# A staged first quarter in stages of 1, 2, 2, 3, 4 and 4 k tiles, with one modulation chunk lent a weight buffer

## The chip, the cores and the metric

One core of a Trainium2 chip runs the kernel. The metric is the device time of one execution in microseconds (us). The profile and the trace come from one profiled execution.

## What is computed

One layer of a flow-matching trunk over 128 context tokens and 256 latent tokens, all in fp32 with D = 2048. Nine modulation vectors per token kind come from `silu(c) @ w_ada + b_ada`; two feed-forward halves stand around a mixer:

```python
def swiglu_sublayer(x, g, w_gate, w_up, w_down, shift, scale, gate):
    h = rms_norm(x, g) * (1 + scale) + shift
    f = (jax.nn.silu(h @ w_gate) * (h @ w_up)) @ w_down
    return x + 0.5 * gate * f

m_ctx = adaln(c_ctx, w_ada[l], b_ada[l])
m_lat = [m[:, None, :] for m in adaln(c, w_ada[l], b_ada[l])]
x_ctx = swiglu_sublayer(x_ctx, ffn1_norm[l], ffn1_w_gate[l], ffn1_w_up[l], ffn1_w_down[l],
                        m_ctx[0], m_ctx[1], m_ctx[2])
...
x_ctx = mixer_output(x_ctx, a, gm, out_norm_a[l], out_norm_b[l], w_out[l], m_ctx[5])
x_ctx = swiglu_sublayer(x_ctx, ffn2_norm[l], ffn2_w_gate[l], ffn2_w_up[l], ffn2_w_down[l],
                        m_ctx[6], m_ctx[7], m_ctx[8])
```

The latent tokens go the same way with neighbourhood attention. Everything that the change touches lies in the first feed-forward half, and there in the first 250 us.

## The kernel before

**Products.** Tokens (384) are the moving columns, with two more columns that carry the shift while the row norm is not known yet (386). Each fp32 product is done as three: weights are split into a high part `whi` (a cast on ACT, line 250) and a low part `wlo` (a subtraction on DVE, line 251), activations into `hh` and `hl`, and `three` (lines 279 to 284) issues `wlo x hh`, `whi x hl`, `whi x hh` into one accumulation bank. A weight chunk W is 1 MB; its two halves are split and used one after the other. A half holds two k tiles of 128 rows by four output columns of 128, so 24 products. I call the n-th half of the kernel slot n, from 0 on. Four pairs of `whi` and `wlo` exist (`NWP`), three buffers `raw` for chunks from HBM (`NRAW`).

**Modulation.** The shift and scale of the first norm (vectors 0 and 1) have to be known before `hh` can be made. They come from 32 chunks A of `w_ada`, 1 MB each, multiplied on TensorE with `silu(c)` as 32-column weights (`ada_chunk`, line 345). When all chunks of a unit of k tiles are through, DVE copies the sums (line 352), four-column products turn them into columns (`ada_unit`, line 364), DVE adds the bias (369) and makes the scale (388), ACT makes `hh` (`raw_hi`, 502) and DVE `hl` (`raw_lo`, 507). Chunks A have two buffers `rawa` (`NADA`) and, at the start, two of the `raw` buffers.

**The staged quarter** (`first_quarter_staged`). Of the hidden columns of the first feed-forward half, the first quarter has six groups. So that products can start before all modulation is known, they run in stages over k tiles (`BLOCKS`, line 39): (0, 2), (2, 4), (4, 6), (6, 8), (8, 12), (12, 16). In each stage all six groups are multiplied with the stage's k tiles. Each group has four accumulation banks of the five of the pool `acc`; at the end of a group's stage `after` evicts them: in the first stage by copies, alternately on ACT (line 720) and DVE (718), in later stages by additions on DVE to the partial sums (724). Before the first slot four chunks A are done; behind each of slots 0 to 27 one more (`ADA_AFTER`, lines 773 and 774), and the columns of a finished unit follow behind the next slot (`settle`).

**What sets the order.** Each engine runs its instructions in the order of the program. `half` (line 262) first splits weights ahead, then runs what `later` has put at this slot's number: loads of x (line 1166), the squares for the row norm (`squares`, lines 1168 and 1169: four squares on ACT and, on DVE, additions to `ssq`, line 455) at slots 9, 12, 16 and 22, the norm at 24. `pump` (line 183) issues loads in the order of use as buffers come free: weight chunks and the first six chunks A on SP's queue, later chunks A on POOL's. A load on a queue that waits for its buffer holds up those behind it.

Of the kernel before, what the change touches and what calls it, by code (L numbers as in the profile page):

```python
# [8 lines left out]
F32 = mybir.dt.float32  # L9
# [6 lines left out]
P = 128  # L16
D = 2048
KT = D // P
# [6 lines left out]
CW = 512  # L25
CK = 4
# [12 lines left out]
BLOCKS = ((0, 2), (2, 4), (4, 6), (6, 8), (8, 12), (12, 16))  # L39
NPE = 0  # L40
ADA_UNITS = tuple(((0, k0, k1), (1, k0, k1)) for k0, k1 in BLOCKS) + ((tuple((2, k, k + 4) for k in range(0, NPE, 4)),) if NPE else ())
ADA_AFTER = (1,) * (28 + NPE)
NSEL = 4

# [70 lines left out]
class Kernel:  # L115
# [4 lines left out]
    def setup(self):  # L120
# [28 lines left out]
        self.freed = {"W": 0, "A": 0}  # L149
        self.next_split = 0  # L150
# [6 lines left out]
        self.room = 2  # L157
# [25 lines left out]
    def pump(self):  # L183

        nc = self.nc
        room = {"W": self.room, "A": NADA}
        while True:
            can = [self.order[k][n] for k, n in self.issued.items()
                   if n < min(len(self.order[k]), self.freed[k] + room[k])]
            if not can:  # L190
                return
            c = min(can)
            k = self.kinds[c]
            if k == "A":
                raw = self.start.tile([P, CK * CW], F32, tag="rawa", name="rawa", bufs=NADA)
                src = self.a["wada_s"][self.issued[k]]
            else:
                raw = self.wp.tile([P, CK * CW], F32, tag="raw", name="raw", bufs=NRAW)
                src = self.a["ws"][self.issued[k]]
            (nc.gpsimd if k == "A" and self.issued[k] >= 6 else nc.sync).dma_start(out=raw, in_=src)  # L200
            self.raw[c] = raw
            self.issued[k] += 1

    def first_loads(self):

        nc = self.nc
        na = 2 * BLOCKS[0][1]
        xin = lambda k, n: nc.sync.dma_start(out=self.xall[:, k:k + n, :], in_=self.a["xT"][:, k:k + n, :])  # L210
        cols = CK * CW
        order = self.order["A"][:na - 1] + [self.order["W"][0], self.order["A"][na - 1]]
        for c in order:
            k = self.kinds[c]
            i = self.issued[k]
            if k == "A" and i < NADA:
                raw = self.start.tile([P, cols], F32, tag="rawa", name="rawa", bufs=NADA)
            else:
                raw = self.wp.tile([P, cols], F32, tag="raw", name="raw", bufs=NRAW)
            self.raw[c] = raw  # L220
            self.issued[k] += 1
            src = self.a["wada_s" if k == "A" else "ws"][i]
            if k == "W":
                w_raw, w_src = raw, src
                nc.sync.dma_start(out=raw[:, 0:1024], in_=src[:, 0:1024])
            elif i < na - 1:
                nc.sync.dma_start(out=raw, in_=src)
                if i == 1:
                    nc.sync.dma_start(out=self.par, in_=self.a["par"])
                    xin(0, 2)  # L230
            else:
                for c0 in range(0, cols, 512):
                    nc.sync.dma_start(out=raw[:, c0:c0 + 512], in_=src[:, c0:c0 + 512])
                nc.sync.dma_start(out=w_raw[:, 1024:cols], in_=w_src[:, 1024:cols])
                self.lent = set(self.order["A"][NADA:na])
        self.freed["A"] = na - NADA
        self.freed["W"] = NADA - na
# [19 lines left out]
    def done(self, c):  # L257
        del self.raw[c]
        self.freed["W" if c in self.lent else self.kinds[c]] += 1
        self.pump()  # L260
# [65 lines left out]
    def ada_chunk(self):  # L326
# [16 lines left out]
        for q in range(nsub):  # L343
# [3 lines left out]
                             stop=done and q >= nsub - 4, tile_position=(0, r))  # L347
        self.done(c)
# [355 lines left out]
    def first_quarter_staged(self):  # L704
# [38 lines left out]
        for st, (k0, k1) in enumerate(BLOCKS):  # L743
            for pairs in stage_halves(st):
# [4 lines left out]
                if slot == 0:  # L749
                    for kk, u in order:  # L750
                        if kk == 0:
                            banks[pairs[0][0], u] = self.bank(u)
                    for w, x, i in ((hi, self.hh, 0), (hi, self.hl, 1), (lo, self.hh, 2)):
                        for kk, u in order:
                            w0 = kk * CW + u * P
                            nc.tensor.matmul(banks[pairs[0][0], u][:, :TS], lhsT=w[:, w0:w0 + P],  # L756
                                             rhs=x[:, kk, :], start=i == 0 and kk == 0, stop=i == 2 and kk == 1)
                    for u in range(4):
                        after(st, pairs[0][0], u, banks.pop((pairs[0][0], u)))
                    order = []  # L760
                for kk, u in order:
# [362 lines left out]
    def run(self):  # L1124
# [15 lines left out]
        with ExitStack() as st:  # L1140
# [3 lines left out]
            self.ada_rows()  # L1144
            self.first_loads()
            xin = lambda k, n=4: nc.sync.dma_start(out=self.xall[:, k:k + n, :], in_=a["xT"][:, k:k + n, :])
            self.gh, self.gl = {}, {}
            for _ in range(2 * BLOCKS[0][1] - 1):
                self.ada_chunk()
            self.ahead(1)  # L1150
            self.ada_chunk()
            self.settle()
            self.ahead(2)
            self.pump()
            xin(2, 2)
# [10 lines left out]
            for k, sl in ((4, 6), (8, 12), (12, 18)):  # L1166
                self.later(sl, lambda k=k: xin(k))
# [3 lines left out]
            one = [(2, k) for k in range(NPE, KT)] + [(j, k) for j in (3, 4) for k in range(KT)]  # L1171
# [11 lines left out]
            self.later(31 + NPE, switch)  # L1183
# [188 lines left out]
```

## Time and profile before

| | |
|---|---|
| median of 3 runs | 2826.48 us (2826.29 to 2827.67) |
| time of the profiled execution | 2826.2 us |
| its span, first to last instruction | 2824.1 us |
| PE busy | 2797.0 us (99%) |
| PE's weight loads (PEld) | 2711.1 us (96%) |
| DVE, ACT, POOL busy | 65%, 36%, 7% |
| mean granted clock of TensorE | 0.997 of full |
| HBM read | 511.88 MB, 185 GB/s over the span |

In the profile's rows a line starts with its start and its busy time in microseconds; `out<-in` are the program's tiles; in brackets stands the idle time ahead of it on its engine and what ended it. L345 is line 345 of the kernel before. PE is TensorE's products, PEld its weight loads, SPq and POOLq the queues that issue transfers. A matmul of fp32 tiles stands as two pieces, so x16 at line 345 are eight products; products overlap, so the distance of their starts counts, not their length.

### The profile page before, as it was taken

The page shows a single profiled execution, that of the slowest core. Times are in us where ns is not written, and L with a number is a line of the kernel's source. Part 1 is how long each engine was busy: PE and PEld are TensorE (multiplying, and loading weights), DVE is VectorE, ACT ScalarE, POOL GpSimd, SP SyncE. Part 2 cuts the span into 40 slices and gives each one's busy share as a digit, 9 for nine tenths or more (in the row PEclk, how much of TensorE's full clock was granted, in tenths as well). Part 3 has the DMA queues.
Part 4 walks back from the last instruction along what each step waited for, and adds up shares of the span by engine and source line. Part 5 has one row for each costly group of instructions (what it writes and reads, how often), then busy time and mean ns, then how long its engine had stood idle before and what let it go on. Part 6 is the DMA issues. An engine that isn't in the chain of part 4 may idle for free.

```text
span 2824.1 us, 39182 instructions
## 1 busy us (share of the span) xinstructions
PE 2797.0 (99%) x15984; PEld 2711.1 (96%) x15984; DVE 1841.8 (65%) x2887; ACT 1015.3 (36%) x1454; POOL 187.4 (7%) x302
## 2 busy tenths in 40 slices
PE   8999999999999999999999999999999999999997
PEld 6889999999999999988888999999999999999997
DVE  4767889798999798765566877554444543333335
ACT  3345432322322244543344445333333223322342
POOL 0031011011111010000000000000000000000000
PEclk9999999999999999999999999999999999999999
DMA  8854676666667675454333653444444433333432
GB/s 349 311 190 166 219 251 240 237 239 241 250 241 253 246 257 197 147 170 141 125 120 116 256 222 137 149 159 162 165 155 151 163 127 129 125 121 138 157 132 80
DMA packets 100035, 524.89 MB, mean 186 GB/s; under 512 B 11024, under 2 KB 18832, under 8 KB 55056
## 3 DMA queue, kind: packets, MB, share of 16 engines
q1 hardware_dynamic: 62224, 371.39, 36.0%
q0 software_dynamic: 37632, 151.01, 15.6%
q8 instruction: 125, 2.05, 0.3%
q14 instruction: 54, 0.44, 0.0%
HBM read 511.88 MB, written 10.49 MB: 185 GB/s over the span
## 4 chain that ended last, share of the span: by engine, by line
PE 99%; DVE 0%; DMA 0%; SPq 0%; ACT 0%; issue 0%; DVEq 0%
PE acc L282 24%; PE acc L284 24%; PE acc L283 24%; PE mp L282 7%; PE mp L284 7%; PE mp L283 6%; PE acc L307 2%; PE acc L308 2%; PE acc L309 2%; PE mp L345 1%; PE mp L858 0%; PE mp L908 0%; PE mp L938 0%; DMA raw<-wada_s 0%; DVE x L1240 0%; PE acc L756 0%
## 5 line engine op out<-in xcount | busy, mean ns | idle before, releaser
L251 DVE TENSOR_TENSOR wlo<-raw,whi 128x1024 fp32r<-128x1024 f32 x640 | 784.5, 1227 | 808.5 <-ACT whi L250 808.1
L250 ACT CAST whi<-raw 128x1024 fp32r<-128x1024 f32 x640 | 670.6, 1050 | 1425.0 <-PE mp L284 1149.9
L282 PE MATMUL acc<-hh,wlo 128*128 128x384 f32 (+1 forms) x2744 | 933.5, 340 | 0.0
L284 PE MATMUL acc<-hh,whi 128*128 128x384 f32 (+1 forms) x2744 | 927.6, 338 | 0.0
L283 PE MATMUL acc<-hl,whi 128*128 128x384 f32 (+1 forms) x2744 | 925.6, 337 | 0.0
L282 PEld LDWEIGHTS acc<-hh,wlo 128*128 128x128 f32 x2744 | 516.6, 188 | 25.5 <-issue 11.3
L283 PEld LDWEIGHTS acc<-hl,whi 128*128 128x128 f32 x2744 | 518.0, 189 | 0.8
L284 PEld LDWEIGHTS acc<-hh,whi 128*128 128x128 f32 x2744 | 516.6, 188 | 0.0
L282 PE MATMUL acc<-gh,wlo 128*128 128x384 f32 x1056 | 357.6, 339 | 0.0
L283 PE MATMUL acc<-gl,whi 128*128 128x384 f32 x1056 | 354.3, 336 | 0.0
L284 PE MATMUL acc<-gh,whi 128*128 128x384 f32 x1056 | 352.8, 334 | 0.0
L436 DVE CUSTOM_DVE_ANT_0 scr<-adaw,csb,par 128x1024 bf16<-128x1024 f32 x224 | 287.3, 1282 | 4.4
L436 DVE CUSTOM_DVE_ANT_0 scr<-adaw,csb,m 128x1024 bf16<-128x1024 f32 x224 | 287.3, 1282 | 4.2
L284 PE MATMUL mp<-hh,whi 128*128 128x384 f32 (+1 forms) x704 | 237.8, 338 | 0.0
L282 PE MATMUL mp<-hh,wlo 128*128 128x384 f32 (+1 forms) x704 | 237.2, 337 | 0.0
L283 PE MATMUL mp<-hl,whi 128*128 128x384 f32 (+1 forms) x704 | 237.0, 337 | 0.0
L421 POOL DMA_DIRECT2D adaw<-wada_t x224 | 118.5, 529 | 1447.9 <-DVE m L436 1352.8
L284 PEld LDWEIGHTS acc<-gh,whi 128*128 128x128 f32 x1056 | 198.5, 188 | 0.0
L283 PEld LDWEIGHTS acc<-gl,whi 128*128 128x128 f32 x1056 | 198.3, 188 | 0.0
L282 PEld LDWEIGHTS acc<-gh,wlo 128*128 128x128 f32 x1056 | 198.0, 188 | 0.0
L283 PEld LDWEIGHTS mp<-hl,whi 128*128 128x128 f32 x704 | 132.7, 189 | 0.0
L282 PEld LDWEIGHTS mp<-hh,wlo 128*128 128x128 f32 x704 | 132.5, 188 | 0.0
(170 smaller groups left out, 2238.5 us busy)
## 6 DMA issues: line engine op xcount, KB each, us to landing
raw<-ws SPq DMA_DIRECT2D x319, 1024.0 KB, 4.9
adaw<-wada_t POOLq DMA_DIRECT2D x224, 512.0 KB, 4.0
rawa<-wada_s POOLq DMA_DIRECT2D x26, 1024.0 KB, 5.9
csb<-crow POOLq DMA_DIRECT2D x6, 1024.0 KB, 7.9
keep<-x SPq DMA_DIRECT2D x8, 768.0 KB, 6.8
rawa<-wada_s SPq DMA_DIRECT2D x4, 1024.0 KB, 8.7
bias<-bias SPq DMA_DIRECT2D x16, 256.0 KB, 4.9
xo<-xT SPq DMA_DIRECT2D x16, 192.0 KB, 5.5
```

The costliest lines, as they stand in the source:

```text
L250: nc.scalar.copy(hi, src)
L251: nc.vector.tensor_sub(lo, src, hi.bitcast(F32))
L282: nc.tensor.matmul(o, lhsT=wl, rhs=xh, start=first, stop=False)
L283: nc.tensor.matmul(o, lhsT=wh, rhs=xl, start=False, stop=False)
L284: nc.tensor.matmul(o, lhsT=wh, rhs=xh, start=False, stop=last)
L307: nc.tensor.matmul(o, lhsT=xh, rhs=wl, start=first and kk == 0, stop=False)
L308: nc.tensor.matmul(o, lhsT=xl, rhs=wh, start=False, stop=False)
L309: nc.tensor.matmul(o, lhsT=xh, rhs=wh, start=False, stop=last and kk == 1)
L345: nc.tensor.matmul(self.ada_bank[r:r + 32, :cols], lhsT=self.csil[:, nsub * kc + q, w0:w0 + 32], rhs=raw[:, q * cols:(q + 1) * cols], star ...
L421: self.nc.gpsimd.dma_start(out=t, in_=self.a["wada_t"][j - 2, kt, kh])
L436: nc.vector.tensor_tensor_reduce(out=scr, in0=t, in1=self.csb[:, v, :], scale=1.0, scalar=init, op0=ALU.mult, op1=ALU.add, accum_out=acc)
```

## The change

Stages are now (0, 1), (1, 3), (3, 5), (5, 8), (8, 12), (12, 16). Units of modulation are the same ranges, with the fourth cut in two, (5, 6) and (6, 8). Only two chunks A come before slot 0; two follow each of slots 0 and 1, none slot 2, and one each of slots 3 to 28. Stage one has one k tile, so that a half holds two groups, each with three products a bank; stage four has three, so that by turns a half holds two k tiles of one group, the last of one and the first of the next, and two of the next. A finished unit's columns are settled in the middle of the next half, behind its fourth triple. The fifth chunk A (A4, counted from 0) goes into one of the three `raw` buffers, which now are taken from a list of free ones; the weight chunks have one buffer of room at the start instead of two. x is loaded in smaller pieces. Around the first chunks `fill` issues products of `ones` into a bank that nobody reads: five behind A0, one behind each quarter of A1, four behind the columns.

```diff
-BLOCKS = ((0, 2), (2, 4), (4, 6), (6, 8), (8, 12), (12, 16))
-NPE = 0
-ADA_UNITS = tuple(((0, k0, k1), (1, k0, k1)) for k0, k1 in BLOCKS) + ((tuple((2, k, k + 4) for k in range(0, NPE, 4)),) if NPE else ())
-ADA_AFTER = (1,) * (28 + NPE)
+BLOCKS = ((0, 1), (1, 3), (3, 5), (5, 8), (8, 12), (12, 16))
+UNITS = ((0, 1), (1, 3), (3, 5), (5, 6), (6, 8), (8, 12), (12, 16))
+LENT = 4
+ADA_UNITS = tuple(((0, k0, k1), (1, k0, k1)) for k0, k1 in UNITS)
+ADA_AFTER = (2, 2, 0) + (1,) * 26
+FILL = (5, 1, 1, 4)
...
-        self.room = 2
+        self.room = 1
...
-            can = [self.order[k][n] for k, n in self.issued.items()
-                   if n < min(len(self.order[k]), self.freed[k] + room[k])]
+            can = [self.order[k][n] for k, n in self.issued.items() if n < len(self.order[k]) and
+                   (self.free if k == "A" and n == LENT else
+                    n - (k == "A" and n > LENT) < self.freed[k] + room[k] and (k == "A" or self.free))]
...
+            if k == "A" and self.issued[k] == LENT:
+                raw = self.raw_buf(c)
+                src = self.a["wada_s"][self.issued[k]]
...
             elif i < na - 1:
                 nc.sync.dma_start(out=raw, in_=src)
-                if i == 1:
-                    nc.sync.dma_start(out=self.par, in_=self.a["par"])
-                    xin(0, 2)
+                xin(0, 1)
             else:
+                nc.sync.dma_start(out=self.par, in_=self.a["par"])
                 for c0 in range(0, cols, 512):
...
+    def fill(self, n):
+        for _ in range(n):
+            self.nc.tensor.matmul(self.idle[:, :P], lhsT=self.ones, rhs=self.ones, start=True, stop=True)
...
+            if (q + 1) % (nsub // 4) == 0 and q < nsub - 1:
+                self.fill(between)
...
                 if slot == 0:
-                    for kk, u in order:
-                        if kk == 0:
-                            banks[pairs[0][0], u] = self.bank(u)
+                    for u in range(4):
+                        banks[pairs[0][0], u] = self.bank(u)
                     for w, x, i in ((hi, self.hh, 0), (hi, self.hl, 1), (lo, self.hh, 2)):
-                        for kk, u in order:
-                            w0 = kk * CW + u * P
-                            nc.tensor.matmul(banks[pairs[0][0], u][:, :TS], lhsT=w[:, w0:w0 + P],
-                                             rhs=x[:, kk, :], start=i == 0 and kk == 0, stop=i == 2 and kk == 1)
+                        for u in range(4):
+                            nc.tensor.matmul(banks[pairs[0][0], u][:, :TS], lhsT=w[:, u * P:(u + 1) * P],
+                                             rhs=x[:, 0, :], start=i == 0, stop=i == 2)
...
-                    order = []
-                for kk, u in order:
+                    order = order[4:]
+                for at, (kk, u) in enumerate(order):
+                    if at == 4:
+                        self.settle()
...
-            for _ in range(2 * BLOCKS[0][1] - 1):
+            for n in FILL[:2 * BLOCKS[0][1] - 1]:
                 self.ada_chunk()
+                self.fill(n)
             self.ahead(1)
-            self.ada_chunk()
+            self.ada_chunk(FILL[-3])
+            self.fill(FILL[-2])
             self.settle()
+            self.fill(FILL[-1])
             self.ahead(2)
+            self.room = 2
             self.pump()
-            xin(2, 2)
+            xin(1, 2)
...
-            for k, sl in ((4, 6), (8, 12), (12, 18)):
-                self.later(sl, lambda k=k: xin(k))
+            for k, n, sl in ((3, 2, 2), (5, 3, 5), (8, 4, 11), (12, 4, 17)):
+                self.later(sl, lambda k=k, n=n: xin(k, n))
```

The order in which instructions stand moves at three places of the staged quarter.

First, SP's queue behind the loads of the start, before (`rawa` and `wada_s` are chunks A, `ws` weight chunks; the first two rows are A4 and A5, then W1 and W2):

```order
L200 DMA rawa<-wada_s 128x2048 [waits DMAHW4_49,PE_49]
L200 DMA rawa<-wada_s 128x2048 [waits DMAHW5_49,PE_49]
L200 DMA raw<-ws 128x2048 [waits DMAHW6_49,PE_49]
L200 DMA raw<-ws 128x2048 [waits DMAHW2_49,DMAHW1_49,DMAHW7_49,DMAHW0_49,PE_49]
L1146 DMA x<-xT 128x768
L200 DMA raw<-ws 128x2048 [waits DMAHW3_49,DVE_49]
```

and with the change (A2, A3, A4, W1, W2, x, W3, A5, W4):

```order
L211 DMA rawa<-wada_s 128x2048 [waits DMAHW2_49,PE_49]
L211 DMA rawa<-wada_s 128x2048 [waits DMAHW5_49,DMAHW6_49,DMAHW3_49,DMAHW7_49,DMAHW0_49,PE_49]
L211 DMA raw<-wada_s 128x2048 [waits DMAHW4_49]
L211 DMA raw<-ws 128x2048
L211 DMA raw<-ws 128x2048 [waits DMAHW1_49,DVE_49]
L1171 DMA x<-xT 128x768
L211 DMA raw<-ws 128x2048 [waits DMAHW5_49,DVE_49]
L211 DMA rawa<-wada_s 128x2048 [waits DMAHW2_49,PE_49]
L211 DMA raw<-ws 128x2048 [waits DMAHW6_49,DVE_49]
```

A chunk A now stands behind three weight chunks, and the third of them waits for DVE, which frees W1's buffer with the second subtraction of W1.

Second, ACT's casts and copies around slots 0 and 1, before (the casts of `raw_167` are W1, that of `raw_191` is W2):

```order
L250 CAST whi_187<-raw_118 128x1024 [waits DMAHW3_49]
L720 COPY part_gh0_223<-acc_195 128x386 [waits PE_49]
L720 COPY part_gh1_227<-acc_197 128x386 [waits PE_49]
L250 CAST whi_231<-raw_167 128x1024 [waits DMAHW6_49]
L250 CAST whi_235<-raw_167 128x1024
L250 CAST whi_241<-raw_191 128x1024 [waits DMAHW7_49,Activation_49]
L720 COPY part_gh2_263<-acc_256 128x386 [waits PE_49]
L720 COPY part_gh3_281<-acc_274 128x386 [waits PE_49]
```

and with the change (W1 is `raw_196`, W2 `raw_198`):

```order
L744 COPY part_gh0_218<-acc_202 128x386 [waits PE_49]
L744 COPY part_gh1_222<-acc_204 128x386 [waits PE_49]
L744 COPY part_gh2_230<-acc_226 128x386 [waits PE_49]
L744 COPY part_gh3_242<-acc_238 128x386 [waits PE_49]
L262 CAST whi_250<-raw_196 128x1024 [waits DMAHW5_49]
L262 CAST whi_254<-raw_196 128x1024
L262 CAST whi_260<-raw_198 128x1024 [waits DMAHW6_49,PE_49,Activation_49]
L744 COPY part_gh4_289<-acc_285 128x386 [waits PE_49]
L744 COPY part_gh5_301<-acc_297 128x386 [waits PE_49]
L744 COPY part_gh6_313<-acc_309 128x386 [waits PE_49]
L744 COPY part_gh7_325<-acc_321 128x386 [waits PE_49]
```

Ahead of slot 1's copies (the rows behind the third cast) stand the same three casts; the copies of a half in stage one are now four on ACT instead of two, since each bank is evicted after three products.

Third, slot 16. PE before, and with the change (in each fence the start of the half):

```order
L282 MATMUL acc_1103<-hh_87,wlo_958 128x386 [waits DVE_49]
L283 MATMUL acc_1103<-hl_88,whi_957 128x386 [waits Activation_49]
L284 MATMUL acc_1103<-hh_87,whi_957 128x386
L282 MATMUL acc_1103<-hh_87,wlo_958 128x386
L283 MATMUL acc_1103<-hl_88,whi_957 128x386
L284 MATMUL acc_1103<-hh_87,whi_957 128x386
L282 MATMUL acc_1111<-hh_87,wlo_958 128x386 [waits DVE_49]
```

```order
L298 MATMUL acc_1079<-hh_87,wlo_973 128x386 [waits Activation_49]
L299 MATMUL acc_1079<-hl_88,whi_972 128x386
L300 MATMUL acc_1079<-hh_87,whi_972 128x386
L298 MATMUL acc_1135<-hh_87,wlo_973 128x386 [waits DVE_49]
L299 MATMUL acc_1135<-hl_88,whi_972 128x386
L300 MATMUL acc_1135<-hh_87,whi_972 128x386
L298 MATMUL acc_1086<-hh_87,wlo_973 128x386
L299 MATMUL acc_1086<-hl_88,whi_972 128x386
L300 MATMUL acc_1086<-hh_87,whi_972 128x386
L298 MATMUL acc_1143<-hh_87,wlo_973 128x386 [waits DVE_49]
```

and DVE in the same slot with the change:

```order
L263 TENSOR_TENSOR wlo_1114<-raw_819,whi_1113 128x1024 [waits Activation_49]
L479 TENSOR_TENSOR ssq_201<-ssq_201,sq_1119 128x384 [waits Activation_49]
L479 TENSOR_TENSOR ssq_201<-ssq_201,sq_1122 128x384 [waits DVE_49,Activation_49]
L479 TENSOR_TENSOR ssq_201<-ssq_201,sq_1125 128x384 [waits DVE_49,Activation_49]
L479 TENSOR_TENSOR ssq_201<-ssq_201,sq_1128 128x384 [waits DVE_49,Activation_49]
L748 TENSOR_TENSOR part_gh0_218<-part_gh0_218,acc_1079 128x386 [waits PE_49]
L748 TENSOR_TENSOR part_gl0_220<-part_gl0_220,acc_1086 128x386 [waits PE_49]
```

Where a bank took six products in a row, banks of two groups alternate after three: `acc_1079` to `acc_1100` stay open from slot 15, `acc_1135` takes the fifth bank, and `acc_1143` the one that DVE empties in the row `part_gh0_218`, which stands behind the four adds.

## Rows read from the trace of the kernel before

**Rows 1.** The page, part 1: busy time, share of the span, instructions.
```profile
PE 2797.0 (99%) x15984; PEld 2711.1 (96%) x15984; DVE 1841.8 (65%) x2887; ACT 1015.3 (36%) x1454; POOL 187.4 (7%) x302
```

**Rows 2.** Waits of PE: total us, times, longest us.
```profile
PE mp L345 <- DMA rawa<-wada_s: 6.7, 2, 6.2
PE mp L345 <- DMA raw<-wada_s: 2.9, 1, 2.9
PE acc L756 <- ACT hh L502: 1.4, 1, 1.4
```

**Rows 3.** Timeline of the start, PE and PEld.
```profile
17.73 0.14 PEld L345 LDWEIGHTS mp<-raw,csil 128*32 128x32 f32 x4 [0.47 <-DMA raw<-wada_s]
...
20.85 3.31 PE L756 MATMUL acc<-hh,whi 128*128 128x386 f32 x8 [1.35 <-ACT hh L502]
...
27.07 1.07 PE L345 MATMUL mp<-rawa,csil 128*32 128x256 f32 x16
...
28.07 0.44 PE L282 MATMUL acc<-hh,wlo 128*128 128x386 f32 x1
...
37.92 1.07 PE L345 MATMUL mp<-rawa,csil 128*32 128x256 f32 x16
```

**Rows 4.** Windows: length, busy us of the engines, granted clock, DMA share, GB/s.
```profile
23.00:24.00 1.00, 1.00 (x5) 1.00 (x5) 0.69 (x1) 0.00 (x0) 0.00 (x0) 0.50 0.97 410
...
25.00:26.00 1.00, 1.00 (x8) 1.00 (x7) 0.00 (x0) 0.00 (x0) 0.00 (x0) 1.00 1.11 459
```

**Rows 5.** Transfers, 0 to 60 us in 40 slices of 1.5 us.
```profile
GB/s 0 104 377 399 431 367 375 421 320 388 337 452 421 421 421 437 431 421 404 448 410 415 410 421 415 426 431 322 426 98 49 306 426 421 418 352 371 279 164 410
```

**Rows 6.** Timelines of SP and POOL: issue of W1 and W2, and of A6.
```profile
15.43 3.30 SPq L200 DMA_DIRECT2D raw<-ws  x2
...
28.49 0.67 POOL L200 DMA_DIRECT2D rawa<-wada_s  x1 [27.18 <-PE mp L345]
```

**Rows 7.** Issue to landing, us, of transfers issued at 15.43, 28.49 and 44.75.
```profile
raw<-ws SPq DMA_DIRECT2D x1, 1024.0 KB, 10.9
...
rawa<-wada_s POOLq DMA_DIRECT2D x1, 1024.0 KB, 7.6
...
rawa<-wada_s POOLq DMA_DIRECT2D x1, 1024.0 KB, 5.1
```

**Rows 8.** Timeline of ACT around slot 1, which starts at 28.07.
```profile
27.20 2.00 ACT L250 CAST whi<-raw 128x1024 fp32r<-128x1024 f32 x2
29.41 1.05 ACT L250 CAST whi<-raw 128x1024 fp32r<-128x1024 f32 x1 [0.21 <-DMA raw<-ws]
30.36 0.48 ACT L720 COPY part_gh<-acc 128x386 f32<-128x386 f32 x1
```

**Rows 9.** Timeline of DVE in slot 16.
```profile
110.50 1.23 DVE L251 TENSOR_TENSOR wlo<-raw,whi 128x1024 fp32r<-128x1024 f32 x1 [0.52 <-ACT whi L250]
111.64 2.54 DVE L455 TENSOR_TENSOR ssq<-ssq,sq 128x384 f32<-128x384 f32 x4
114.10 0.55 DVE L724 TENSOR_TENSOR part_gh<-part_gh,acc 128x386 f32<-128x386 f32 x1
```

**Rows 10.** Timeline of PE at the start of slot 16.
```profile
109.31 1.07 PE L345 MATMUL mp<-rawa,csil 128*32 128x512 f32 x8
110.31 0.44 PE L282 MATMUL acc<-hh,wlo 128*128 128x386 f32 x1
...
110.94 0.34 PE L282 MATMUL acc<-hh,wlo 128*128 128x386 f32 x1
...
111.47 0.34 PE L282 MATMUL acc<-hh,wlo 128*128 128x386 f32 x1
```

**Rows 11.** Timeline of DVE behind a unit of four k tiles.
```profile
138.26 2.97 DVE L507 SCALAR_TENSOR_TENSOR hl<-x,s,hh 128x128 fp32r<-128x128 f32 x8 [0.31 <-ACT hh L502]
141.69 1.23 DVE L251 TENSOR_TENSOR wlo<-raw,whi 128x1024 fp32r<-128x1024 f32 x1 [0.45 <-ACT whi L250]
```

**Rows 12.** Timeline of PE, the same unit's columns.
```profile
136.36 0.95 PE L364 MATMUL mp<-par,adasb 128*128 128x4 f32 x8
```

More of the change, by code (lines that the diff above doesn't have):

```diff
@@ L149, in setup @@
         self.freed = {"W": 0, "A": 0}
+        self.free = deque(range(NRAW))
+        self.buf = {}
         self.next_split = 0
@@ L193, in pump @@
             k = self.kinds[c]
-            if k == "A":
+            if k == "A" and self.issued[k] == LENT:
+                raw = self.raw_buf(c)
+                src = self.a["wada_s"][self.issued[k]]
+            elif k == "A":
                 raw = self.start.tile([P, CK * CW], F32, tag="rawa", name="rawa", bufs=NADA)
@@ L197, in pump @@
             else:
-                raw = self.wp.tile([P, CK * CW], F32, tag="raw", name="raw", bufs=NRAW)
+                raw = self.raw_buf(c)
                 src = self.a["ws"][self.issued[k]]
@@ L202, in pump, with raw_buf @@
             self.issued[k] += 1
+    def raw_buf(self, c):
+        i = self.free.popleft()
+        self.buf[c] = i
+        return self.wp.tile([P, CK * CW], F32, tag=f"raw{i}", name="raw", bufs=1)
     def first_loads(self):
@@ L218, in first_loads @@
             else:
-                raw = self.wp.tile([P, cols], F32, tag="raw", name="raw", bufs=NRAW)
+                raw = self.raw_buf(c)
             self.raw[c] = raw
@@ L234, in first_loads @@
                 nc.sync.dma_start(out=w_raw[:, 1024:cols], in_=w_src[:, 1024:cols])
-                self.lent = set(self.order["A"][NADA:na])
-        self.freed["A"] = na - NADA
-        self.freed["W"] = NADA - na
+        self.lent = {self.order["A"][LENT]}
     def ahead(self, n=NWP):
@@ L258, in done @@
         del self.raw[c]
-        self.freed["W" if c in self.lent else self.kinds[c]] += 1
+        k = self.kinds[c]
+        if c in self.buf:
+            self.free.append(self.buf.pop(c))
+        if c not in self.lent:
+            self.freed[k] += 1
         self.pump()
@@ L324, in ada_rows, with ada_chunk @@
         nc.scalar.activation(self.csil[:, :, NSEL - 2:NSEL], ct, AF.Silu)
-    def ada_chunk(self):
+    def fill(self, n):
+        for _ in range(n):
+            self.nc.tensor.matmul(self.idle[:, :P], lhsT=self.ones, rhs=self.ones, start=True, stop=True)
+    def ada_chunk(self, between=0):
         nc = self.nc
@@ L1144, in run @@
             self.ada_rows()
+            self.idle = self.misc()
             self.first_loads()
@@ L1170, in run @@
             self.later(24, norm)
-            one = [(2, k) for k in range(NPE, KT)] + [(j, k) for j in (3, 4) for k in range(KT)]
+            one = [(2, k) for k in range(KT)] + [(j, k) for j in (3, 4) for k in range(KT)]
             two = [(j, k) for j in (5, 6, 7) for k in range(KT)]
@@ L1181, in switch @@
                 self.wide = True
-            self.later(31 + NPE, switch)
+            self.later(len(ADA_AFTER) + 2, switch)
             n1, n2, n3, n4 = SP
```

## The prediction

> **What bounds the kernel now.** The page's first part comes first: TensorE is busy 99% of the span [rows 1]. The waits of PE then show where the missing time lies: outside the tail, the only waits longer than a microsecond are at the start, for the modulation chunks and for the first `hh` [rows 2]. So a wait that is put anywhere into the stream of products lengthens the kernel one for one, and the only thing to win is an earlier first product. That first product starts at 20.85 us, 3.1 us after the last quarter of the fourth chunk let PE go on at 17.73; its half takes 6.2 us to 27.07, where 24 products at full clock take 4.27 (a triple starts every 0.53 us [rows 10], eight triples a half) [rows 3]. [...]
>
> I write A0, A1, ... for the modulation chunks and W0, W1, ... for the weight chunks, in the order of use (1.05 MB each), and slot n for the n-th half.
>
> **The start.** Before the first product now lie A0, one tile of x, half of W0, `par` and A1: 2.99 MB with `ct`. The transfer row gives what was moved by any time: 1.5 us times the sum of its figures, 3.08 MB by 10.5 us, 7.85 by 22.5, 9.15 by 25.5, 11.06 by 30 [rows 5]. A transfer lands when it and all before it are moved and about 0.5 MB of followers too: W1 of before, with which 8.96 MB are asked for, was issued at 15.43 [rows 6] and landed 10.9 us later [rows 7], at 26.3, with 9.5 moved. So A1 is there at 3.5 MB: 11.5 us. One k tile instead of two takes some 0.4 us off the 3.1 behind it: first product at 14.2, 6.7 us earlier. The filling matmuls lie in PE's waits for transfers and in the wait for `hh`; I cost them at nothing (five, then one to four, in gaps of over a microsecond [rows 2]), and give them the 1.9 us of clock. Against that, two chunks more (1.0 us each [rows 3]) run inside the stream.
>
> Without new waits the third half with its six chunks would end at 14.2 + 3 x 4.27 + 4 x 1.05 + 0.5 (columns, gaps) = 31.7. In before, three halves and six chunks were done at 37.92, where the next chunk starts [rows 3]. The most that can be won is 6.2 us.
>
> **What is late next.** Slot 0 ends at 18.5, A2 and A3 (landed by the same curve at 15.9 and 18.4) at 20.75. From here the transfers decide.
>
> - *Slot 1.* On ACT three casts stand ahead of slot 1's copies, the third for W2 (the second piece of the order above). In before the same order cost nothing: the cast waited for W2 until 29.41 and the first copy ran at 30.36, 2.3 us into the half [rows 8]; each bank then took six products and five banks lasted 5.3 us. Now a bank gets three products: the five are full 2.67 us into the slot, at 23.4. W2 is the 8.76th MB, so by the curve it lands at 25.9; but POOL issues A6 as soon as A3 is used, at 20.9, where in before it did so at 28.49 [rows 6]. That chunk landed in 7.6 us beside SP's loads and a later one in 5.1 with less beside it [rows 7]: 2.5 us longer, as much as its own 1.05 MB takes at 0.42 MB/us, so I let it take half of the rate from 22.8 on. W1 then lands at 24.0 and W2 at 28.2. Cast 1.05, copy 0.48 [rows 8]: PE goes on at 29.8 after 6.4 us of standing. Slot 1 ends at 31.4, A4 at 32.4.
> - *The sixth chunk.* A5 stands behind W3 on SP's queue, and W3 waits for both splits of W1: 24.0 + 2.1 for the casts, 1.23 for the last subtraction [rows 9]: 27.4. A5 is issued at 28.2. Up to it 12.3 MB are asked for with A6, so 12.8 moved: 34.1 if nothing stood still; as the queue runs nearly dry before W3, I take 35.2. A5 ends at 36.3, slot 2 with the unit's columns in its middle at 40.9.
>
> That is 3.0 us later than the 37.92 of before: the earlier start is used up and more. Bounds: with A6 behind everything and no dry queue A5 lands when 11.75 MB are moved, at 31.6, and slot 2 ends at 37.3, 0.6 us earlier than before; with the lower clock behind the long wait it is 4.5 later.
>
> **The stage of three k tiles** (slots 15 to 23). Its middle halves, slots 16, 19 and 22, hold the last k of one group and the first of the next, by turns (the third piece of the order). Four banks are open, the next group's first takes the fifth, and its second must wait until DVE has evicted the first. That eviction can begin 0.6 us into the half. But DVE has first the subtraction of the weights and, in slots 16 and 22, the four adds of the squares, which keep their slot numbers. The trace has that very stretch: in slot 16 of before the half starts at 110.31 [rows 10], DVE subtracts at 110.50, adds to 114.1 and only then evicts until 114.65 [rows 9]. There it cost nothing, since a bank took 1.07 us. Now PE wants the bank 1.6 us into the half and gets it at 4.3: +2.7 in slot 16. In slot 19 without adds the subtraction ends some 1.3 us in, the eviction at 1.85: +0.25. In slot 22 the adds follow the eight `hl` of the unit of four k tiles, which now settles in the middle of slot 21: in before the columns start at 136.36, `hl` runs 138.26 to 141.2, the next subtraction starts at 141.69, 5.3 us behind the columns [rows 11, 12]. Counted from slot 21's start: columns 2.14, subtraction 7.4, 3.6 more to the end of the adds [rows 9], eviction 11.55. Slot 22 starts at 6.25 (4.27, columns 0.9, chunk 1.07) and wants the bank at 7.85: +3.7. Together +6.65; I allow 5 to 8, half a microsecond either way for each.
>
> **The rest.** The unit of one k tile (5 to 6) uses sixteen narrow products a chunk; chunks of eight and of four cost the same 1.0 us [rows 3, 10], so nothing, at most 0.6. A seventh unit adds no columns. Moved settling adds no work. Stages of four and everything behind them keep their order; PE stays full there, so nothing of a delay is given back. For the clock behind the new gaps (6.4, 2.8, 2.7 and 3.7 us) no row has the like: the trace shows the lower level only at the start, before PE had ever been full. I take 0.5; bounds 0 and 1.9 for each gap, as slot 0 paid [rows 3].
>
> Sum: +3.0 + 6.65 + 0.5 = +10.2 on the profiled execution's 2826.2 (its span 2824.1; the median of the runs is 0.3 above it): 2836.5 us, slower by 0.36%.
>
> **Rivals.**
> 1. *The middle halves do not wait for the adds.* If the evictions in slots 16 and 22 came before the adds, the second term vanishes: 2826.2 + 3.5 = 2829.7. For it: PE's stream never stalled in slot 16 of before. Against it: DVE's order is fixed in the program and the row shows it evicting only at 114.1. It decides if the eviction is over within 1.6 us of the half. This is the side that is not slower. 0.10.
> 2. *A6 does not hold up W2.* A5 lands at 31.6, the first term is -0.6: 2832.3. For it: A6 is the younger transfer. Against it: the 7.6 us. 0.13.
> 3. *Both, or a rate above 0.42 MB/us:* 2825.6, down to the full 6.2 us at 2820. No window of the first 31 us shows a rate that would do it for long [rows 5]. 0.07, of it 0.04 faster.
> 4. *The clock falls in every gap:* four times 1.9 instead of 0.5: 2843.5. For it: the 0.50 at 20.85 after a start of waits. Against it: PE is full between the gaps. 0.08. [...] No row here shows a fall from full clock.
> 5. That the first product is not earlier, since PE's fillers at the lower clock hold up the quarters: it changes little, as W2 and A5 decide.
>
> **Numbers.** The forecast has 0.62, with 0.06 of it below 2832.1. What a measurement of this kernel can tell from no change is about 0.2%, 5.65 us: 2820.8 to 2832.1. Faster 0.04; same: rival 1, the rest of 3, half of 2 and 0.06: 0.25; slower 0.71. The range runs from 2828, which takes in rivals 1 and 2, to 2842.5, which is 2826.2 with the first term at 4.5, the second at 8 and two gaps that cost 1.9 of clock; rival 3 and most of 4 stay out, some 0.15.
>
> **What would show it.** Right: first product near 14 us at clock 1.00; a wait of PE for ACT of some 6 us at about 23 to 30, one for A5 until about 35; in slots 16 and 22 waits of PE for DVE of about 2.7 and 3.7 us; the fourth half at about 41. Wrong: PE full from 14 us on, or no wait for DVE between 100 and 150 us; then the time is 2820 to 2830.

## The result, and the profile after

The changed kernel takes **2842.52 us** (median of 6 runs, 2839.61 to 2843.28), the kernel before 2826.78 in the runs beside it: a ratio of 1.0052 [1.0042, 1.0063], slower by about half a per cent. The profiled execution of the change took 2842.24 us (span 2840.1), against 2826.2 before: +16.0.

Page, part 1, of after:

```profile
PE 2805.7 (99%) x16074; PEld 2719.4 (96%) x16074; DVE 1848.8 (65%) x2892; ACT 1015.3 (36%) x1455; POOL 185.8 (7%) x302
```

Against [rows 1] PE is busy 8.7 us longer. The rows of the 13 fillers add up to 5.8 us, and products at the lower clock take longer (0.32 us from start to start instead of 0.18, see below); of the 90 instructions more, 26 are the fillers (two pieces each) and 64 come from four chunks that are now multiplied in products of half the width. The other 7.3 of the 16.0 us are waits. Waits of PE in after (total us, times, longest):

```profile
PE mp L367 <- DMA rawa<-wada_s: 7.5, 2, 6.4
PE acc L298 <- DVE part_gh L748: 6.1, 2, 3.6
PE acc L298 <- ACT part_gh L744: 4.4, 1, 4.4
PE acc L298 <- ACT hh L561: 0.5, 1, 0.5
```

The chunks cost less than in [rows 2] at the start; three waits are new, for copies of ACT, for additions of DVE, and for one `hh` much later. Timeline of PE at the start (lines have moved: 345 is now 367, 282 is 298; compare [rows 3]):

```profile
13.53 0.42 PE L367 MATMUL mp<-rawa,csil 128*32 128x128 f32 x8
...
16.10 0.97 PE L778 MATMUL acc<-hh,whi 128*128 128x386 f32 x4 [0.35 <-ACT hh L526]
...
20.53 1.93 PE L367 MATMUL mp<-rawa,csil 128*32 128x256 f32 x32
...
29.68 0.69 PE L298 MATMUL acc<-hh,wlo 128*128 128x386 f32 x1 [4.38 <-ACT part_gh L744]
30.17 0.53 PE L299 MATMUL acc<-hl,whi 128*128 128x386 f32 x1
...
32.87 1.94 PE L367 MATMUL mp<-raw,csil 128*32 128x256 f32 x16
35.85 1.93 PE L367 MATMUL mp<-rawa,csil 128*32 128x256 f32 x16 [1.04 <-DMA rawa<-wada_s]
...
47.49 1.07 PE L367 MATMUL mp<-rawa,csil 128*32 128x256 f32 x16
```

The first product stands at 16.10, slot 0 takes 4.4 us at full clock, A2 and A3 run at 20.53 in 1.93 together. Then PE stands 4.38 us in slot 1, for a copy that ACT makes only behind the cast of W2 (timeline of ACT; compare [rows 8]):

```profile
25.02 1.99 ACT L262 CAST whi<-raw 128x1024 fp32r<-128x1024 f32 x2 [4.44 <-DMA raw<-ws]
28.20 1.04 ACT L262 CAST whi<-raw 128x1024 fp32r<-128x1024 f32 x1 [1.19 <-DMA raw<-ws]
29.15 1.24 ACT L744 COPY part_gh<-acc 128x386 f32<-128x386 f32 x3
```

From there a single chunk (A4, then A5) takes 1.93 instead of 1.07, and products start 0.32 us apart instead of 0.18: the clock is at its lower level (0.50, in the windows below). A5 starts at 35.85, when it lands; it was issued at 28.91, behind W3 (timelines of SP and POOL; [rows 6]):

```profile
28.49 0.33 SPq L211 DMA_DIRECT2D raw<-ws  x1
28.91 0.68 SPq L211 DMA_DIRECT2D rawa<-wada_s  x1
```

```profile
22.81 0.67 POOL L211 DMA_DIRECT2D rawa<-wada_s  x1 [21.50 <-PE mp L367]
```

Slots 16 and 22 on PE, each the first product of the second bank, and the late `hh`:

```profile
119.15 0.44 PE L298 MATMUL acc<-hh,wlo 128*128 128x386 f32 x1 [2.53 <-DVE part_gh L748]
...
156.76 0.69 PE L298 MATMUL acc<-hh,wlo 128*128 128x386 f32 x1 [3.56 <-DVE part_gh L748]
157.25 0.53 PE L299 MATMUL acc<-hl,whi 128*128 128x386 f32 x1
157.57 0.52 PE L300 MATMUL acc<-hh,whi 128*128 128x386 f32 x1
...
232.45 0.44 PE L298 MATMUL acc<-hh,wlo 128*128 128x384 f32 x1 [0.47 <-ACT hh L561]
```

DVE meanwhile, in slot 16 and from the `hl` in slot 21 to slot 22 (compare [rows 9, 11]):

```profile
114.94 1.23 DVE L263 TENSOR_TENSOR wlo<-raw,whi 128x1024 fp32r<-128x1024 f32 x1 [4.23 <-ACT whi L262]
116.09 2.54 DVE L479 TENSOR_TENSOR ssq<-ssq,sq 128x384 f32<-128x384 f32 x4
118.54 0.55 DVE L748 TENSOR_TENSOR part_gh<-part_gh,acc 128x386 f32<-128x386 f32 x1
```

```profile
149.14 2.96 DVE L531 SCALAR_TENSOR_TENSOR hl<-x,s,hh 128x128 fp32r<-128x128 f32 x8 [0.31 <-ACT hh L526]
152.56 1.23 DVE L263 TENSOR_TENSOR wlo<-raw,whi 128x1024 fp32r<-128x1024 f32 x1 [0.45 <-ACT whi L262]
153.70 2.54 DVE L479 TENSOR_TENSOR ssq<-ssq,sq 128x384 f32<-128x384 f32 x4
156.16 0.55 DVE L748 TENSOR_TENSOR part_gh<-part_gh,acc 128x386 f32<-128x386 f32 x1
```

The granted clock (second last but one figure) behind two of the waits, in windows as in [rows 4]:

```profile
29.70:32.90 3.20, 3.20 (x13) 2.76 (x13) 2.21 (x4) 1.17 (x3) 0.00 (x0) 0.50 0.88 356
```

```profile
156.70:161.80 5.10, 5.04 (x15) 4.68 (x15) 1.59 (x4) 0.00 (x0) 0.00 (x0) 0.50 0.44 173
```

**Where the 16.0 us lie.** Each slot from 3 on ends with a chunk, so the starts of line 367 (before: 345) date the slots in both traces, and their differences say where time is lost (all but 0.1 of the 16.0):

| stretch | later by |
|---|---|
| up to the chunk behind slot 3 (47.49, before 43.35), and one chunk (1.0) more still owed | 5.1 |
| slots 4 to 15 | 0.3 |
| slot 16 | 2.8 |
| slots 17 to 21 (19 alone: 0.4) | 0.5 |
| slot 22 | 6.1 |
| slot 37: two triples start 1.16 and 0.98 apart instead of 0.53 | 1.1 |
| sum | 15.9 |

The 5.1 include 0.4 for a unit's columns (at 40.58), which the kernel before makes only in slot 4 (at 48.68); slots 4 to 15 lose by as much more than the 0.3.

### The profile page after: what moved, and what is told of

It reads as the page before. It is cut to its first block, busy times and chain, and to the rows that moved or that the text cites. A ratio compares the mean times of both kernels' runs of the same rounds, so it can differ in the third digit from the quotient of the medians.

```text
span 2840.1 us, 39375 instructions
## 1 busy us (share of the span) xinstructions
PE 2805.7 (99%) x16074; PEld 2719.4 (96%) x16074; DVE 1848.8 (65%) x2892; ACT 1015.3 (36%) x1455; POOL 185.8 (7%) x302
## 4 chain that ended last, share of the span: by engine, by line
PE 97%; DVE 1%; DMA 1%; ACT 1%; issue 0%; SPq 0%; DVEq 0%; ACTq 0%
PE acc L298 24%; PE acc L300 23%; PE acc L299 23%; PE mp L298 6%; PE mp L300 6%; PE mp L299 6%; PE acc L323 2%; PE acc L324 2%; PE acc L325 2%; PE mp L367 1%; PE mp L882 0%; DMA rawa<-wada_s 0%; PE mp L932 0%; PE mp L962 0%; DMA raw<-ws 0%; DVE wlo L263 0%
```

## Experiments

My theory after the result: PE's waits add up, and each has its own cause: the squares' adds ahead of an eviction (slots 16, 22), A5's place behind three weight chunks (start), the late `hh` (slot 37), plus the lower clock behind some of the waits. The median of the kernel before, beside them, was 2827.0 to 2827.3, against 2826.8 beside the change, so a difference to 2842.52 can be off by half a microsecond; the runs of the change itself lie 3.7 us apart. Where a gain is smaller than that, the trace has to show it.

**e1, the squares at slots 15 and 20.**

```diff
-            for k, sl in ((0, 9), (4, 12), (8, 16), (12, 22)):
+            for k, sl in ((0, 9), (4, 12), (8, 15), (12, 20)):
```

> Edit: the squares of slots 16 and 22 run at slots 15 and 20, halves that need no bank before an eviction. Theory (banks): in slots 16 and 22 PE waits because the first eviction stands behind the four adds on DVE, so the wait of 2.5 us in slot 16 goes, that of 3.6 in slot 22 falls to about 1.2 (the hl of the unit of four tiles remains ahead), and the clock no longer falls behind it, which gives back 2.1: about 7 us in all, 2835.5. Rival (load): DVE has too much to do in this stage, and the adds only move the wait to the slots they go to: total of PE's waits for DVE still about 6 us, time within 1.5 us of 2842.5.

2833.52 us (2832.91 to 2838.1), ratio 1.0026 [1.0016, 1.0036]: 9.0 less. Waits of PE:

```profile
PE acc L298 <- DVE part_gh L748: 1.1, 1, 1.1
```

The wait of slot 16 is gone, that of slot 22 is 1.1, and the clock stays at 1.00 there. The chunk behind slot 28 starts at 186.60 instead of 195.24. 2.5 + 2.5 of the 8.6 are the two waits, some 2.2 the clock in slot 22; the last 1.4 arose before slot 4, where in this execution A5 ran at full clock, which the edit doesn't touch. Two of the ten runs lie apart, at 2836.9 and 2838.1; why is open. At slots where no bank is short the same adds cost nothing that the trace shows (the 1.1 is the only wait for DVE's additions that is left): it is their place, not DVE's load.

**e2, middle halves not alternating.** With all four products of the ending group first, the next group's second bank is wanted 1.07 us later.

```diff
-                if k1 - k0 > 1:
+                if k1 - k0 > 1 and pairs[0][0] == pairs[1][0]:
```

> Edit: in the middle halves the first group's four banks are finished before the second group's begin, instead of by turns. Theory (banks): the second group's second bank is wanted 1.07 us later (at 2.67 instead of 1.6 us into the half), so the waits fall from 2.5 to about 1.45 us in slot 16, from 3.6 to about 2.5 in slot 22, from 0.24 to none in slot 19: 2.4 us less, and 2.1 more if the clock holds behind slot 22: 2838 to 2840. Rival (load): the same adds are done by the same engine, waits and time as in the change, 2842.5.

2839.01 us (2837.55 to 2840.16), ratio 1.0043 [1.0029, 1.0058]: 3.5 less.

```profile
PE acc L298 <- DVE part_gh L748: 3.9, 2, 2.5
```

The longest wait fell from 3.6 to 2.5, by just the 1.07, slot 19's is gone. By the chunks' starts slot 16 is 1.05 us shorter, slot 19 0.3 and slot 22 1.9; of the last 1.1 are the wait and the rest is the clock, which fell again, here behind a wait of 2.48 us, but for fewer products. So the alternation is the smaller part of the cause, the adds ahead of the eviction the larger.

**e3, fillers ahead of the two waiting products.**

```diff
+                    if at == 1 and slot in (16, 22):
+                        self.fill(10 if slot == 16 else 14)
```

> Edit: fillers that nobody reads, ten in slot 16 and fourteen in slot 22, ahead of the product that waits for its bank (about 2.1 and 3.0 us at full clock). Theory (clock): the wait itself stays, as PE is busy with fillers inside it and goes on at the same time, but the clock is 1.00 behind slot 22 instead of 0.50, so the fifteen products there start 0.18 us apart instead of 0.32: 2.1 us less, about 2840.4, and runs no longer differ by 2.6 us among themselves. Rival: the lower clock there has another cause; then the clock is 0.50 again and the time 2842 to 2843, or later by what the fillers take.

2840.17 us (2839.47 to 2841.29), ratio 1.0048 [1.0033, 1.0063]: 2.3 less, although nothing that PE waits for comes earlier. The fillers stand behind the first triple of the half, two triples ahead of the product that waits, and leave it a wait of 0.44 us in slot 22. The chunk behind slot 22 starts at 160.02 instead of 161.89, and the clock stays at 1.00:

```profile
158.00:160.00 2.00, 2.00 (x12) 1.76 (x10) 0.96 (x2) 0.00 (x0) 0.00 (x0) 1.00 0.69 291
160.02 1.07 PE L367 MATMUL mp<-rawa,csil 128*32 128x512 f32 x8
```

Slot 22 itself is 2.3 us shorter (0.55 had been lost at the chunk behind slot 13, which waited for its transfer in this execution). So the lower clock behind slot 22's wait was a cost of its own, about 2 us.

**e4, no fillers at the start.**

```diff
-FILL = (5, 1, 1, 4)
+FILL = (0, 0, 0, 0)
```

> Edit: no filling matmuls at the start. Theory (transfers): the first product comes at 15 to 16.5 us and its half runs at the lower clock (1.9 us longer), but W2 and A5 still land at 28.2 and 35.8, so the sixth chunk starts at 35.9 as with the change, and the time is within 0.7 us of 2842.5. Rival (fillers): the fillers hold up the quarters of A1 and everything behind; without them the whole stream is 1 to 2 us earlier, 2841.

2844.5 us (2843.74 to 2845.04), ratio 1.0063 [1.0048, 1.0078]: 2.0 more, which I had not expected. The first product stands at 15.89, hardly earlier than 16.10, but slot 0 starts at a lower rate (its first four products take 1.65 us instead of 0.97; the granted-clock column reads 1.00 from 16 to 20 us) and A2 starts at 21.70 instead of 20.53; A5 landed at 37.14, 1.3 later, though it was issued no later (28.56). Why it landed later is open; A6 beside it was issued later too, at 23.98 instead of 22.81. In this kernel the clock fell behind slot 16's wait, of the same length as in after, and not behind slot 22's:

```profile
121.52 0.69 PE L298 MATMUL acc<-hh,wlo 128*128 128x386 f32 x1 [2.52 <-DVE part_gh L748]
```

```profile
122.00:124.00 2.00, 2.00 (x8) 2.00 (x8) 0.14 (x1) 0.00 (x0) 0.00 (x0) 0.50 1.02 430
```

**e5, W2's cast behind slot 1's copies.**

```diff
-                    self.ahead()
+                    self.ahead(3 if slot == 0 else NWP)
```

> Edit: the cast of W2 no longer stands ahead of slot 1's copies on ACT, but behind them (three splits ahead in slot 0 instead of four). Transfers untouched. If the transfers set the end of slot 2 (my theory), PE gets its bank some 2.1 us earlier (at about 27.6 instead of 29.7), but A5 still lands at about 35.9, so that the wait for A5 grows by as much, to some 2 to 3 us: 2842.5, within 0.7 (2841.8 to 2843.2). If the order on ACT sets it, slot 2 ends 2 us earlier: 2840.5.

2842.45 us (2841.62 to 2843.14), ratio 1.0054 [1.004, 1.0068]: unchanged. PE's wait for ACT fell from 4.4 to 2.1, and A5 still started at 35.76:

```profile
35.76 1.94 PE L367 MATMUL mp<-rawa,csil 128*32 128x256 f32 x16 [4.61 <-DMA rawa<-wada_s]
```

All that slot 1 won went into the wait for A5. The wait of 4.4 us, the longest that the change makes in the stream, does not set the time as long as A5 comes when it does.

**e6, A6 on SP's queue behind A5.**

```diff
-            (nc.gpsimd if k == "A" and self.issued[k] >= 6 else nc.sync).dma_start(out=raw, in_=src)
+            (nc.gpsimd if k == "A" and self.issued[k] >= 7 else nc.sync).dma_start(out=raw, in_=src)
```

> Edit: A6 is issued on SP's queue behind A5 instead of on POOL's queue as soon as A3 is used; later chunks on POOL as before. If A6 holds up W2 and A5 (my theory), W2 lands at 26 to 26.5 instead of 28.2, slot 1 goes on at about 27.5 instead of 29.7, A5 lands at 33.5 to 34.5 instead of 35.9, and the kernel takes 1.5 to 2.5 us less: 2840 to 2841. If A6, the younger transfer, does not hold them up, W2 still lands at about 28.2, A5 at about 35.9, and the time is 2842.5, within 0.7; if A6 itself is now late, slot 3 waits for it and the time is above that.

2841.12 us (2840.46 to 2842.72), ratio 1.005 [1.0037, 1.0064]: 1.4 less, which the runs alone cannot tell from no change; W2 and A5 came later than expected. The third cast, W2's, starts 1.2 us earlier, of which 0.5 is W1's earlier landing (24.48; it was issued as much earlier in this execution):

```profile
27.03 1.04 ACT L262 CAST whi<-raw 128x1024 fp32r<-128x1024 f32 x1 [0.56 <-DMA raw<-ws]
```

W3, which takes W1's buffer, was issued 0.5 earlier too (27.94 instead of 28.49), and A5 started at 35.31, again 0.5 earlier: A5 has gained nothing beyond W1's head start. The other part is that A5 ran at full clock in this execution (1.07 instead of 1.93). So A6's price on W2 was at most some 0.6 us, where I gave it 2.3, and on A5 none that this execution shows. Even the 0.6 is weak: between W1's cast and W2's lie 2.55 us here, and 2.75 (e4) to 3.47 (e1) in the traces with A6 on POOL's queue and the casts in this order.

**e7, A5 too in a `raw` buffer, ahead of W1.** A6 and A7 go on SP's queue, and the splits ahead are held to 1, 2 and 2 in slots 0 to 2, so that no cast of a late chunk stands ahead of a copy.

```diff
-LENT = 4
+LENT = (4, 5)
...
-            (nc.gpsimd if k == "A" and self.issued[k] >= 6 else nc.sync).dma_start(out=raw, in_=src)
+            (nc.gpsimd if k == "A" and self.issued[k] >= 8 else nc.sync).dma_start(out=raw, in_=src)
...
-                    self.ahead()
+                    self.ahead((1, 2, 2)[slot] if slot < 3 else NWP)
```

> Edit: A5 too is lent one of the raw buffers, and so is issued right behind A4 and ahead of W1; A6 and A7 go on SP's queue, later chunks on POOL's; splits ahead in slots 0, 1, 2 are held to 1, 2, 2, so that no cast of a late chunk stands ahead of a copy. If the early loads' order is what costs the start its gain (my theory: A5 behind three weight chunks, A6 beside them, W2's cast ahead of the copies), the waits in slot 1 and for A5 go, slot 2 ends at 34 to 36 instead of about 43, and the time is 7 to 9 us less: 2833.5 to 2835.5. If the transfers as a whole are too slow for an earlier start whatever their order (rival), another chunk comes late in place of A5 and the time stays within 2 us of 2842.5.

2835.25 us (2833.6 to 2836.62), ratio 1.0028 [1.0018, 1.0039]: 7.3 less. Timeline of PE:

```profile
26.66 1.93 PE L367 MATMUL mp<-raw,csil 128*32 128x256 f32 x32
29.90 0.44 PE L298 MATMUL acc<-hh,wlo 128*128 128x386 f32 x1 [1.30 <-DVE wlo L263]
...
39.02 1.07 PE L367 MATMUL mp<-rawa,csil 128*32 128x256 f32 x16
...
56.65 1.07 PE L367 MATMUL mp<-rawa,csil 128*32 128x256 f32 x16 [1.21 <-DMA rawa<-wada_s]
```

A4 and A5 run together right behind slot 1, which doesn't wait at all; slot 2 waits 1.3 us for W2's split instead. The chunk behind slot 3 starts at 39.02 instead of 47.49, 8.5 us earlier. The rival has a part in it: the chunk behind slot 6 now waits 1.21 us for its transfer, and from there on 7.1 us are left. So the transfers were fast enough for most of an earlier start; their order was not. Which of the three parts of the edit does it alone is not shown: e5 and e6 had two of them one at a time and won nothing and little, and A5's place alone was not run.

**e8, all together**: e7, e1, e2, and the last unit's `hh` made earlier (e9's edit).

> Edit: the lent A5 with its order of loads, the squares at slots 15 and 20, the middle halves of stage four not alternating between their two groups, and the last unit's hh made at slots +0, 1, 3 and 5 instead of every second slot. If the four causes are separate and the kernel's time is the sum of PE's waits (my theory), the gains add up: 7 to 9 at the start, 9 to 10 in slots 16, 19 and 22 with their clock, 1 at slot 37, in all 17 to 20 off 2842.5: 2823 to 2826, no slower than the kernel before (2826.8). If the causes cover each other (a wait that is removed leaves DVE or a transfer late at the next place), less than 14 us come back and the time stays above 2828.5.

2824.71 us (2823.83 to 2825.57), ratio to the kernel before 0.9991 [0.9982, 1.0]: 17.8 less than the change, and level with the kernel before. Waits of PE:

```profile
PE mp L367 <- DMA rawa<-wada_s: 8.2, 4, 6.2
PE acc L298 <- DVE wlo L263: 1.3, 1, 1.3
PE acc L778 <- ACT hh L526: 0.3, 1, 0.3
PE mp L709 <- DVE ssq L494: 0.3, 1, 0.3
```

Two of the four waits for chunks lie behind the start: 0.85 us behind slot 6 and, new, one behind slot 19:

```profile
128.27 1.07 PE L367 MATMUL mp<-rawa,csil 128*32 128x512 f32 x8 [0.74 <-DMA rawa<-wada_s]
```

The causes are nearly separate. Of e1's 9.0 us 1.4 lie at the start, where e7 has them too; the other 7.6, e7's 7.3, 1.1 for `hh`, and 1.4 that the order of the banks still cost in slots 19 and 22 make 17.4. The new wait of 0.74 us suggests that transfers begin to limit what more could be won.

**e9, the last unit's `hh` at slots +0, 1, 3, 5.**

```diff
-                    self.later(self.slot + 2 * i, lambda kt=k0 + i: self.make_h(self.rs, kt))
+                    self.later(self.slot + (0, 1, 3, 5)[i], lambda kt=k0 + i: self.make_h(self.rs, kt))
```

> Edit: of the last unit of modulation (four k tiles) the hh are made at slots +0, 1, 3 and 5 behind its columns instead of every second slot; all else as in the changed kernel. If PE's wait of 0.5 us for hh in slot 37 and the slower products around it are real cost (my theory), that wait goes and the time is 0.5 to 1.0 less: 2841.5 to 2842.0; the products behind slot 36 stand 0.53 us apart without a gap. If the wait only moves to another place behind it, the time is 2842.5, within 0.5, and the trace has a new wait behind slot 37.

2839.35 us (2837.84 to 2844.18), ratio 1.0047 [1.0034, 1.0061]: 3.2 less by the medians, more than the wait can give. The trace splits it: the wait for `hh` is gone and all triples around slot 37 are 0.53 apart (1.1); the other 2.2 is that in this execution the clock did not fall behind slot 22, after the same wait, which the edit does not touch:

```profile
156.84 0.44 PE L298 MATMUL acc<-hh,wlo 128*128 128x386 f32 x1 [3.56 <-DVE part_gh L748]
```

```profile
157.00:159.00 2.00, 2.00 (x12) 2.00 (x13) 0.81 (x2) 0.00 (x0) 0.00 (x0) 1.00 0.98 389
```

Its five runs lie at 2837.8 to 2839.4 and at 2842.9 and 2844.2; those of after at 2839.6 and 2840.1 and at 2842.2 to 2843.3. A fall that comes in some executions would part them so. Only profiled runs have a trace, but every run has its mean granted clock: 0.996 or 0.997 in the lower runs of both kernels, 0.994 or 0.995 in the higher, and five microseconds at 0.50 take 0.0009 off the mean. So the higher runs did run longer at the lower clock; that it was in slot 22 is argued.

**e10, fillers in slot 1's wait and ahead of A5.**

```diff
+                    if at == 5 and slot == 1:
+                        self.fill(14)
...
+                    if slot == 1 and n == 1:
+                        self.fill(10)
```

> Edit: 14 filling products in slot 1 ahead of the product that waits for its bank, and 10 ahead of A5; transfers and all else as in the changed kernel. If the lower clock between 29.7 and 39 us is cost of its own and comes from PE's standing (my theory), the clock stays 1.00, A5 starts where it did (35.9, its transfer decides) but takes 1.07 us instead of 1.93, and the first products of slot 2 are 0.18 us apart instead of 0.32: 1.5 us less, 2841.0 (2840.3 to 2841.7). If the clock there costs nothing, since the transfers cover it, the time is 2842.5, within 0.5. If the fillers themselves hold up PE (24 in all, 0.28 us each at full clock), slot 2 ends later and the time is up to 2 us above.

2842.34 us (2840.99 to 2844.58), ratio 1.0055 [1.004, 1.0069]: no difference that can be told. The expected gain is there at first, and is lost again in this execution:

```profile
36.41 1.07 PE L367 MATMUL mp<-rawa,csil 128*32 128x256 f32 x16 [1.19 <-DMA rawa<-wada_s]
...
46.55 1.07 PE L367 MATMUL mp<-rawa,csil 128*32 128x256 f32 x16
```

The clock stayed full, A5 took 1.07 (landing 0.6 later in this execution), and the chunk behind slot 3 started 0.9 us earlier. But the chunk behind slot 13 had to wait 0.52 us for its transfer: it started at 102.53, 0.35 earlier than in after. The chunk behind slot 23 started at 167.37 against 167.32, since the lower clock of slot 22 reached 0.4 us further. The wait at slot 13 does not come from the earlier start: e3, only 0.14 us ahead there, has it too (0.48), and e1 and e6, which were 1.4 and 2.1 us ahead, do not. The clock at the start is worth 1.5 us on the spot, and e1 and e6, where A5 happened to run at full clock, kept their lead up to slot 22; e10's own runs don't show it.

## Why the prediction was right, and where its sum was short

Slower was right, with the predicted mechanism: products wait for banks, for A5, and for DVE behind the adds. The time came out 6 us above the forecast, on the upper edge of the range (2842.5), with three of the six runs above it; that the median fell just there is luck.

- **The start, +3.0: measured 5.1.** W2's landing (28.2), the restart in slot 1 (29.8 forecast, 29.68), A5 behind W3 behind W1's splits (issue 28.2, measured 28.91; start 35.2, measured 35.85) came near the steps, although the first product came at 16.10, not 14.2. That it "changes little, as W2 and A5 decide" (rival 5) was right, and 6.4 us of standing became 4.38; that the fillers are the reason was not, as without them it stood at 15.89 (e4). W2's landing on the very number is luck in part: W1 came a microsecond later than forecast (25.02 for 24.0), and A6 cost at most some 0.6 and not 2.3 (e6). What the term left out is the clock: about 1.5 of the 2.1, the rest the 0.65 of the later A5. Of the parts of the cause, the cast's place counted for nothing alone (e5) and A6 for a quarter of what I took at most (e6); with A5 moved as well 7 us came back (e7), so slot 1's wait and A5's covered each other.
- **The fillers, "costed at nothing".** The quarters of A1 were worked off at PE's pace, the last at 13.53, and the fillers took some time: without them the first product came 0.2 us earlier. But slot 0 then started at the lower rate (1.65 us for four products instead of 0.97), and the kernel took 2.0 us more (e4).
- **The middle halves, +6.65: measured 7.1 without the clock** (slot 16 2.8 for 2.7, slot 19 0.4 for 0.25, slot 22 3.9 for 3.7). Counting DVE's rows from before gave these terms; e1 and e2 confirm both halves of the step. Rival 1 is out.
- **The clock, +0.5: measured 3.7** (1.5 at the start, 2.2 in slot 22). This is the mis-sized term: half of the 5.8 us that the sum lacked. I had given the four gaps an eighth of a microsecond each with bounds of 0 and 1.9; two of the four paid about the upper bound. The reason I gave, that the lower level stands "only at the start, before PE had ever been full", misread the trace of before, which holds a fall that no row shows:

```profile
18.40:20.85 2.45, 0.61 (x4) 0.52 (x4) 1.35 (x7) 1.05 (x4) 0.00 (x0) 1.00 1.01 426
22.00:23.00 1.00, 1.00 (x5) 1.00 (x4) 0.55 (x2) 0.43 (x1) 0.00 (x0) 0.50 0.99 418
```

  The clock had risen before the first product: from 17.5 on the chunk's products took 0.38 to 0.41 us, against 0.63 before. (Until then the column reads 1.00 too, so the products' times have to be read beside it.) PE then stood for most of 18.40 to 20.85, and slot 0 ran at 0.50 to 0.55 until 24 us. So the 1.9 us of slot 0 (6.2 us, where 24 products at full clock take 4.27), which I took for a clock that had not yet risen, were the price of a fall behind a wait, and rival 4 deserved more than 0.08. In after the clock fell to 0.50 behind the waits of 4.38 and 3.56 us too; behind the same 3.56 in e4 and e9 it held at 1.00.
- **"Stages of four and everything behind them keep their order; PE stays full": failed**, by 1.1 us. The last unit is settled in the middle of slot 29 instead of behind slot 28, and its four `hh`, at every second slot from there, come about a slot later, so the last one now comes when slot 37 already wants it.
- **"Nothing of a delay is given back"** held for all the waits of after. An earlier start can be taken back in part, though: e7's by the chunk behind slot 6 (1.2 of 8.4 us).
- **The prices of rivals 2 and 3** (2832.3 and 2825.6) leave out the 0.5 for the clock, which rival 1 has; nothing hangs on it.

Of the parts that the prediction didn't have (late landing 0.65, `hh` 1.1, small delays in slots 4 to 22 together 0.9, clock 3.2) the sum is 5.8, the gap between +10.2 and +16.0.

## What to carry to other kernels

Where TensorE is full, as here (99% of the span), look at what stands ahead of the first eviction behind a stage boundary, in the order of the engine that empties the banks, and move that, before anything else: here it left PE standing 2.53 and 3.56 us for DVE, and moving it took 7.6 us off (e1). When a start is made earlier, follow each load's place in its queue; a chunk that stands behind a load which waits for a buffer can set the time, as A5 did here as far as e7 shows (issued at 28.91, right behind W3 at 28.49; 7.3 us less with A5 ahead of W1 and e7's two other edits), and neither the longest wait on the page nor the engine it names need be what decides (e5). And price a new wait in a full stream with the lower clock behind it as an upper case of its own (here 1.5 us at the start and 2.2 in slot 22), not as a small allowance.

## What the hardware showed that I had not expected

The granted clock after a wait was not settled by the wait's length here. Behind 2.5 us in slot 16 it stayed at 1.00 in after, the products stood as close in e6, e7, e9 and e10 (0.18 us apart), and it fell to 0.50 in e4; behind the same 3.56 us in slot 22 it fell in after, e5, e6, e7 and e10 and stayed in e4 and e9; and in e2 it fell behind 2.48 us. Where it fell, the loss was about 2.2 us in slot 22 (15 products 0.32 instead of 0.18 us apart) and 1.5 at the start. Why it fell in one and not in the other is open. With fillers put into the wait it did not fall: in slot 22 of e3 the window reads 1.00, and in slot 1 of e10 products are 0.18 us apart and A5 takes 1.07 (one trace each).
